# Two decoder layers on one core: the last Strassen product's weight forms emitted earlier, and half of a token tile scaled by ScalarE at the turn of the layers

## The chip, the cores and the metric

The kernel runs on one core of a Trainium2 chip. The metric is device time in microseconds (us) of one execution, given as the median of several runs. The names of the engines are those of the profile: PE is TensorE's matrix product, PEld its weight load, DVE is VectorE, ACT is ScalarE, POOL is GpSimd, SP issues most of the transfers.

## What is computed

Two layers (`DEPTH` = 2) of a decoder trunk on 512 tokens of width 1024, in float32. Cut to what matters here:

```
for l in range(DEPTH):
    a = hybrid_mixer(rms_norm(x, pre_mix_g[l]), ...)            # first product: h @ w_in[l]
    x = x + rms_norm(a, post_mix_g[l])
    c = memory_cross_attention(rms_norm(x, pre_xattn_g[l]), ...)
    x = x + rms_norm(c, post_xattn_g[l])
    hdn = jnp.square(jax.nn.relu(rms_norm(x, pre_mlp_g[l]) @ w_up[l]))   # width 4096
    x = x + rms_norm(hdn @ w_down[l], post_mlp_g[l])
```

`rms_norm(x, g)` is `x * rsqrt(mean(x*x) + 1e-6) * g`. The change lies in the last line, and in the step from there to the first line of the next layer ("the turn of the layers"): the residual x of the first layer is complete, is normalised and transposed, and feeds the second layer's product with `w_in`.

## The kernel before

The tokens are four tiles of 128 rows (t = 0 to 3), and each tile's 1024 columns are two halves of 512 (n = 0, 1). Every float32 operand of a product is kept as a rounded part and a rest (`whi` and `wlo` of a weight, `fh` and `fl` of an activation, `xth` and `xtl` of the transposed input), and one logical product is three matmuls into one PSUM bank (lines 239 to 241: hi x rest, rest x hi, hi x hi). The rounded part is made by ACT and the rest by DVE.

**The down product.** `hdn @ w_down` runs in four passes `qd_` over the inner dimension. In each, a 2 x 2 block product is done with seven products of combined operands. `plan` lists the seven as (number p, PSUM tiles, first, last, destinations). For product p, `right_form(p, B[g])` makes the weight's form for each half g of the pass's inner dimension: where needed DVE subtracts two raw weight blocks into one (line 1036 for p = 4), then `parts_w` (lines 161 to 166) makes `whi` on ACT (line 164) and `wlo` on DVE (line 165). `finish(j)` adds the finished PSUM tile of token tile d + j to the running sums `acc[t][n]` on DVE (line 1104). In the last pass (`end`) the order of `plan` is 1, 2, 5, 6, 3, 7, 4, and a completed half of `acc` goes through `done(t, n)`: sum of squares on ACT (`sumsq`, line 372, output `mss`), times the gain on DVE (line 1042). Once both halves of a token tile are there, `add_post_norm` follows: a small DVE operation (`pnm`, line 417), a power on POOL (`pnr`, line 139), and two DVE operations that make the new residual (`xs`, line 420). Product 4 is the last of the pass. It completes tiles 2 and 3, and its matmuls are the ones named `we` at the end of a layer, 24 of them, for j = 0 and 1 and g = 0 and 1.

**The turn.** In the first layer `done` then stores the tile and calls `norm_x(nxh, nxl, t, "n1")` (lines 393 to 407): two sums of squares of `xs` on ACT (line 372), `n1m` on DVE (line 376), the power `n1r` on POOL (line 139), and the two halves `xn` = `xs` times `n1r`, both on POOL (line 405). `put_off` delays the transposes in the emitted program: `transposed` turns each half with four PE transposes (`tp`, line 224), and ACT and DVE split it into `xth` (line 201) and `xtl` (line 203). The second layer's first product (PSUM tiles `ptm`, one for each token tile) needs `xth` and `xtl` of its token tile and the split of `w_in` (`whi` line 192, `wlo` line 197, one 128 x 512 operation per half of a weight tile).

**What sets the order.** The program is emitted in the order of the Python code. A list scheduler of the framework then orders each engine's instructions ahead of time, from its own costs, and each engine runs its list in that order, waiting on semaphores. So the same emitted code can stand in another order on an engine than in the source. Two tiles of PSUM serve the transposes (`tp`), four the tiles `we` and `ptm`.

Of the kernel before, what the change touches and what calls it, by code (L numbers as in the profile page):

```python
# [15 lines left out]
AF = mybir.ActivationFunctionType  # L16
OP = mybir.AluOpType
# [28 lines left out]
def block_kernel(ctx: ExitStack, tc, x, mem, positions, rel_bias, w_in, q_norm_g, w_uq, kv_norm_g,  # L46
# [3 lines left out]
    nc = tc.nc  # L50
# [13 lines left out]
    def unit(name, shape=(128, 512), dt=F32):  # L64
        return un.tile(list(shape), dt, tag="u", name=name)

    def small(name, w):
        return sm.tile([128, 4], F32, tag="sm", name=name)[:, :w]
# [8 lines left out]
    xs = [[None, None] for _ in range(NT)]  # L77
# [133 lines left out]
    def put_off(key, us, fn):  # L211
        late.append((clk[0] + us, key, fn))
# [153 lines left out]
    def feat_major(*a, **k):  # L366
        run(feat_major_steps(*a, **k))

    def sumsq(src, ss, scale=1.0):
        w = src.shape[-1]  # L370
        junk = unit("junk", (128, w))
        nc.scalar.activation(junk, src, AF.Square, scale=scale, accum_out=ss)

    def row_rstd(ms, tag):
        m = small(tag + "m", 1)
        nc.vector.scalar_tensor_tensor(m, ms[0], EPS, ms[1], op0=OP.add, op1=OP.add)
        return rpow(m, tag)

    def transposed(xn, n, dests, t):

        tp = t_ps("tp")
        for j in range(4):
            transpose(tp[:, j * 128:(j + 1) * 128], xn[:, j * 128:(j + 1) * 128], ident)
        tpv = tp.rearrange("p (j c) -> p j c", j=4)
        w = 8 // len(dests)
        for i in range(0, 4, w):
            h, lo = dests[(n * 4 + i) // w]
            k0 = (n * 4 + i) % w
            mw = min(w, 4)
            split_from(h[:, k0:k0 + mw, t * 128:(t + 1) * 128],  # L390
                       lo[:, k0:k0 + mw, t * 128:(t + 1) * 128] if SPLIT else None, tpv[:, i:i + mw, :])

    def norm_x(h, lo, t, tag, fast=()):

        hv = (h[:, 0:4, :], h[:, 4:8, :])
        lv = (lo[:, 0:4, :], lo[:, 4:8, :]) if SPLIT else (None, None)
        ms = small(tag + "ms", 2)
        for n in range(2):
            sumsq(xs[t][n], ms[:, n:n + 1], scale=1.0 / 32.0)
        r = row_rstd((ms[:, 0:1], ms[:, 1:2]), tag)  # L400
        xns = []
        for n in range(2):
            xn = unit("xn")
            eng = nc.vector if n in fast else nc.gpsimd
            eng.tensor_scalar(xn, xs[t][n], r[:, 0:1], 1.0, op0=OP.mult, op1=OP.mult)
            xns.append(xn)
        put_off(("xt", t), DELAY, lambda: [transposed(xns[n], n, list(zip(hv, lv)), t) for n in range(2)])

# [150 lines left out]
    for l in range(DEPTH):  # L559

        if l == 0:
            xth, xtl = new_xt()
            with tc.high_priority():
                norm_x(xth, xtl, 0, "n1", fast=(1,))
                ensure(("xt", 0))
            idle_products(10)

# [304 lines left out]
        xth, xtl = new_xt()  # L872
# [99 lines left out]
        xth, xtl = new_xt()  # L972
# [26 lines left out]
        nxh = nxl = None  # L999
# [25 lines left out]
        def right_form(p, b):  # L1025


            b11, b12, b21, b22 = b
            if p == 5:
                nc.vector.tensor_sub(b11, b12, b11)  # L1030
            elif p == 6:
                nc.vector.tensor_sub(b11, b22, b11)
            elif p == 7:
                nc.vector.tensor_sub(b12, b22, b12)
            elif p == 4:
                nc.vector.tensor_sub(b11, b21, b11)
            return parts_w({1: b11, 5: b11, 6: b11, 2: b21, 7: b12, 3: b22, 4: b11}[p])

        def done(t, n):

            sumsq(acc[t][n], ss[t][:, n:n + 1], scale=1.0 / 32.0)
            nc.vector.tensor_mul(acc[t][n], acc[t][n], gb[n])
            ready_halves[t] += 1
            if ready_halves[t] < 2:
                return
            add_post_norm(acc[t], ss[t], t, out[0] if l == DEPTH - 1 else None)
            if l < DEPTH - 1:
                store_x(t, xsave)
                norm_x(nxh, nxl, t, "n1")

        ready_halves = [0] * NT

        for qd_ in range(4):
            if qd_ == 3 and l < DEPTH - 1:
                nxh, nxl = new_xt()
            F = {p: [] for p in range(1, 8)}
            for g in range(2):
                ra = pp.tile([128, 1280], F32, tag="P", name="ra", bufs=2)[:, 0:1024]
                rb = pp.tile([128, 1280], F32, tag="PT", name="rb", bufs=2)[:, 0:1024]
                ra, rb = [r.rearrange("p (k c) -> p k c", k=2) for r in (ra, rb)]  # L1060

                def ev_up(m, ps, ra=ra, rb=rb):
                    r = (ra, rb)[m // 2][:, m % 2, :]
                    nc.scalar.activation(r, ps, AF.Relu)
                    nc.scalar.activation(r, r, AF.Square)

                feat_major(w_up[l], (qd_ * 2 + g) * 512, 4, NK, G_MLP + 8 * l, xh_f, xl_f, S, ev_up,
                           whole=2 if qd_ == 0 and g == 0 else 0)
                left_forms(F, ra, rb)
            B = [[raw_w(w_down[l], qd_ * 1024 + g * 512 + r * 256, 2, n * 512, 512)  # L1070
                  for r in range(2) for n in range(2)] for g in range(2)]
            A = [pss.tile([128, 512], F32, tag="s", name="wa") for _ in range(2)]
            C = [pst.tile([128, 512], F32, tag="t", name="wc") for _ in range(2)]
            E = [None] * 2
            end = qd_ == 3


            plan = ((1, A, True, False, ((0, 0),)), (5, C, True, False, ((2, 1),)),
                    (6, A, False, False, ((0, 1),)), (2, E, True, True, ((0, 0),)),
                    (7, A, False, False, ((2, 1),)), (3, C, False, True, ((0, 1),)),  # L1080
                    (4, A, False, True, ((2, 0),)))
            if end:
                plan = ((1, A, True, False, ((0, 0),)), (2, E, True, True, ((0, 0),)),
                        (5, C, True, False, ((2, 1),)), (6, A, False, False, ((0, 1),)),
                        (3, C, False, True, ((0, 1),)), (7, A, False, True, ((2, 1), (2, 0))),
                        (4, E, True, True, ((2, 0),)))
            for p, ps, first, last, dsts in plan:
                if ps is E:
                    E[:] = [mm_ps("we") for _ in range(2)]

                def product(g, i, j, w):
                    c = slice(j * 128, (j + 1) * 128)
                    fh, fl = F[p][g]
                    mm(ps[j], fh[:, i, c], fl[:, i, c], w[0][:, i, :], w[1][:, i, :],
                       first and g + i == 0, g + i == 2, not first)

                def finish(j):
                    for d, n in dsts:
                        t = d + j
                        if acc[t][n] is None:  # L1100
                            acc[t][n] = unit("acc")
                            nc.vector.tensor_copy(acc[t][n], ps[j])  # L1102
                        else:
                            nc.vector.tensor_add(acc[t][n], ps[j], acc[t][n])
                        if end and p in (2, 3, 4) or end and p == 7 and n == 1:
                            done(t, n)

                if end and p == 4:
                    w = [right_form(p, B[g]) for g in range(2)]
                    for j in range(2):  # L1110
                        for g in range(2):
                            for i in range(2):
                                product(g, i, j, w[g])
                        finish(j)
                        flush()
                    continue
                for g in range(2):
                    w = right_form(p, B[g])
                    for i in range(2):
                        for j in range(2):  # L1120
                            product(g, i, j, w)
                if end and p == 1:
                    gb = row_bcast(post_mlp_g, l)
                for j in range(2):
                    finish(j)
                if end and p in (2, 5):
                    for t in ((0, 1) if p == 2 else (2, 3)):
                        load_x(t, xmid)
                flush()
        xth, xtl = nxh, nxl  # L1130
# [36 lines left out]
```

## Time and profile before

| | |
|---|---|
| median of 3 runs | 1558.0 us (1557.4 to 1561.02) |
| the profiled execution, own time | 1556.26 us |
| its span in the trace | 1554.5 us |
| PE busy | 1510.6 us, 97% of the span |
| DVE busy | 997.8 us, 64% |
| ACT busy | 818.0 us, 53% |
| POOL busy | 245.1 us, 16% |

Times below are microseconds from the start of the profiled span. The span is 1.8 us shorter than the execution's own time, which is 1.7 us below the median of the runs. A busy share is an average over stages; matmuls overlap by their pipelining, so that consecutive ones start 0.23 us apart although one is listed with 0.39 us. [...]

### The profile page before, as it was taken

How to read it: one execution, taken by the hardware profiler on the slowest of the kernel's cores; microseconds unless marked ns; L12 is line 12 of the kernel's file. 1: busy time of each engine (PE TensorE's matmuls, PEld its weight loads, DVE VectorE, ACT ScalarE, POOL GpSimd, SP SyncE). 2: the span in 40 equal slices, each digit the busy share in tenths (PEclk: the TensorE clock that was granted, in tenths of full speed). 3: DMA queues.
4: the chain of work that ended last, by engine and by line, in shares of the span. 5: the costliest groups of instructions: out<-in, count | busy, mean ns of one | idle time of the engine just before them, and what ended most of it. 6: DMA issues, size and time to landing. Idle time of an engine off the chain costs nothing.

```text
span 1554.5 us, 21284 instructions
## 1 busy us (share of the span) xinstructions
PE 1510.6 (97%) x7861; PEld 1264.8 (81%) x7861; DVE 997.8 (64%) x1780; ACT 818.0 (53%) x1574; POOL 245.1 (16%) x433
## 2 busy tenths in 40 slices
PE   8999999999999999999989999999999999999996
PEld 6777788898898888888768877978988988888885
DVE  5555766456449677685974667654554695949577
ACT  5355766355356364645544566654554554645453
POOL 2133621021020000000121355201111100000000
PEclk9999999999999999999999999999999999999998
DMA  6432223513131506051631322243322324150512
GB/s 237 140 116 69 88 72 105 191 55 122 55 109 57 183 18 190 28 176 48 196 114 51 121 92 79 69 156 129 109 82 68 123 80 137 39 178 14 190 64 72
DMA packets 87404, 164.09 MB, mean 106 GB/s; under 512 B 6230, under 2 KB 12036, under 8 KB 87300
## 3 DMA queue, kind: packets, MB, share of 16 engines
q1 hardware_dynamic: 86724, 161.68, 31.9%
q8 instruction: 62, 1.02, 0.3%
q10 hardware_dynamic: 576, 1.05, 0.2%
q14 instruction: 42, 0.34, 0.1%
HBM read 154.29 MB, written 11.03 MB: 106 GB/s over the span
## 4 chain that ended last, share of the span: by engine, by line
PE 84%; DVE 7%; issue 3%; ACT 2%; DMA 2%; POOL 1%; SPq 0%; DVEq 0%; POOLq 0%; ACTq 0%
PE pfm L240 12%; PE pfm L239 12%; PE pfm L241 12%; PE ptm L239 6%; PE ptm L240 6%; PE ptm L241 6%; PE wa L239 3%; PE wa L240 3%; PE wa L241 3%; PE op L230 3%; PE sp L464 3%; DVE wlo L197 2%; PE ptp L224 2%; PE wc L240 2%; PE wc L241 2%
## 5 line engine op out<-in xcount | busy, mean ns | idle before, releaser
L240 PE MATMUL pfm<-xth,wlo 128*128 128x512 f32 (+1 forms) x896 | 322.4, 360 | 0.6
L239 PE MATMUL pfm<-xtl,whi 128*128 128x512 f32 (+1 forms) x896 | 322.2, 360 | 0.0
L241 PE MATMUL pfm<-xth,whi 128*128 128x512 f32 (+1 forms) x896 | 321.6, 359 | 0.0
L197 DVE SCALAR_TENSOR_TENSOR wlo<-raw,gT,whi 128x512 fp32r<-128x512 f32 (+3 forms) x332 | 229.9, 732 | 131.4 <-ACT whi L192 129.7
L192 ACT ACTIVATE whi<-raw,gT 128x512 fp32r<-128x512 f32 (+2 forms) x324 | 208.9, 697 | 179.8 <-PE pfm L241 87.3
L164 ACT ACTIVATE whi<-raw 128x1024 fp32r<-128x1024 f32 x112 | 118.1, 1060 | 143.0 <-PE pfm L241 52.8
L240 PEld LDWEIGHTS pfm<-xth,wlo 128*128 128x128 f32 x896 | 169.2, 189 | 27.0 <-DVE wlo L197 1.4
L241 PEld LDWEIGHTS pfm<-xth,whi 128*128 128x128 f32 x896 | 169.2, 189 | 25.5 <-issue 0.5
L239 PEld LDWEIGHTS pfm<-xtl,whi 128*128 128x128 f32 x896 | 169.2, 189 | 25.0
L165 DVE TENSOR_TENSOR wlo<-raw,whi 128x1024 fp32r<-128x1024 f32 x112 | 135.0, 1219 | 34.3 <-ACT whi L164 34.3
L139 POOL TENSOR_TENSOR pnr<-pnm,mhalf 128x1 f32<-128x1 f32 x24 | 17.2, 715 | 828.6 <-DVE pnm L417 828.6
L472 POOL TENSOR_SCALAR P<-P,rs 128x128 f32<-128x128 f32 (+3 forms) x128 | 71.4, 562 | 149.3 <-DVE rs L471 78.8
L239 PE MATMUL wa<-wlo,fh 128*128 128x512 f32 x240 | 93.6, 390 | 0.5 <-DVE acc L1102 0.5
L240 PE MATMUL wa<-whi,fl 128*128 128x512 f32 x240 | 93.4, 389 | 0.0
L241 PE MATMUL wa<-whi,fh 128*128 128x512 f32 x240 | 93.4, 389 | 0.0
L470 ACT ACTIVATE P<-P,nm 128x128 f32<-128x128 f32 (+3 forms) x128 | 71.1, 557 | 32.1 <-DVE nm L468 31.3
L185 DVE TENSOR_TENSOR wlo<-raw,whi 128x1024 fp32r<-128x1024 f32 x32 | 39.1, 1223 | 59.3 <-ACT whi L184 58.6
L239 PE MATMUL ptm<-wlo,xth 128*128 128x512 f32 (+2 forms) x192 | 68.3, 357 | 2.2 <-DVE wlo L197 1.8
L184 ACT ACTIVATE whi<-raw 128x1024 fp32r<-128x1024 f32 x32 | 33.9, 1061 | 67.2 <-PE ptm L241 64.5
L240 PE MATMUL ptm<-whi,xtl 128*128 128x512 f32 (+2 forms) x192 | 67.0, 349 | 0.2 <-DVE xtl L203 0.2
L241 PE MATMUL ptm<-whi,xth 128*128 128x512 f32 (+2 forms) x192 | 66.4, 346 | 0.0
L224 PE MATMUL ptp<-ident,P 128*128 128x128 f32 x320 | 50.4, 281 | 4.3 <-ACT PT L491 2.3
(248 smaller groups left out, 3286.9 us busy)
## 6 DMA issues: line engine op xcount, KB each, us to landing
raw<-in_w_up SPq DMA_DIRECT2D x64, 512.0 KB, 4.7
raw<-in_w_down SPq DMA_DIRECT2D x64, 512.0 KB, 4.1
raw<-in_w_in SPq DMA_DIRECT2D x24, 512.0 KB, 4.9
raw<-in_w_xk SPq DMA_DIRECT2D x16, 512.0 KB, 4.7
raw<-in_w_xv SPq DMA_DIRECT2D x16, 512.0 KB, 3.7
raw<-in_w_mix_out SPq DMA_DIRECT2D x16, 512.0 KB, 4.5
raw<-in_w_xq SPq DMA_DIRECT2D x16, 512.0 KB, 6.4
raw<-in_w_xo SPq DMA_DIRECT2D x16, 512.0 KB, 4.2
```

Source lines behind the costliest of these rows:

```text
L164: nc.scalar.activation(hi, raw, AF.Copy)
L165: nc.vector.tensor_sub(lo, raw, hi.bitcast(F32))
L192: weight_parts[:] = [nc.scalar.activation(cols(hi, k, False), cols(raw, k, True), AF.Copy, scale=g).ins]
L197: nc.vector.scalar_tensor_tensor(lv, rv, g, hv, op0=OP.mult, op1=OP.subtract)
L224: ins = nc.tensor.transpose(out_, in_, ident_)
L230: nc.tensor.matmul(ps, lhsT=lhsT, rhs=rhs, start=start, stop=stop)
L239: nc.tensor.matmul(ps, lhsT=lh, rhs=rl, start=first, stop=False, skip_group_check=more)
L240: nc.tensor.matmul(ps, lhsT=ll, rhs=rh, start=False, stop=False, skip_group_check=more)
L241: nc.tensor.matmul(ps, lhsT=lh, rhs=rh, start=False, stop=last, skip_group_check=more)
L464: nc.tensor.matmul(sp[:, :L], lhsT=q[:, i * 128:(i + 1) * 128], rhs=k[:, :L], start=n == 0, stop=n == len(parts) - 1)
L470: nc.scalar.activation(Pi, Pi, AF.Exp, bias=nm[:, i:i + 1], scale=-1.0, accum_out=rs[:, i:i + 1])
L472: nc.gpsimd.tensor_scalar(Pi, Pi, rs[:, i:i + 1], 1.0, op0=OP.mult, op1=OP.mult)
```

## The change

It does two things. In the last pass the two forms of product 4 are emitted behind the matmuls of product 7 and ahead of product 7's `finish`, instead of at the head of product 4. And `norm_x` takes an argument that says who scales the second half: at the turn of the layers that is ACT now (`nc.scalar.activation` with `scale=r`), POOL keeps the first half. At the start of the kernel DVE scales the second half as before; the other calls of `norm_x` keep POOL for both.

```diff
-    def norm_x(h, lo, t, tag, fast=()):
+    def norm_x(h, lo, t, tag, help=None):
...
             xn = unit("xn")
-            eng = nc.vector if n in fast else nc.gpsimd
-            eng.tensor_scalar(xn, xs[t][n], r[:, 0:1], 1.0, op0=OP.mult, op1=OP.mult)
+            if n == 1 and help is nc.scalar:
+                nc.scalar.activation(xn, xs[t][n], AF.Copy, scale=r[:, 0:1])
+            else:
+                eng = nc.gpsimd if n == 0 or help is None else help
+                eng.tensor_scalar(xn, xs[t][n], r[:, 0:1], 1.0, op0=OP.mult, op1=OP.mult)
             xns.append(xn)
...
-                norm_x(xth, xtl, 0, "n1", fast=(1,))
+                norm_x(xth, xtl, 0, "n1", help=nc.vector)
...
-                norm_x(nxh, nxl, t, "n1")
+                norm_x(nxh, nxl, t, "n1", help=nc.scalar)
...
                 if end and p == 4:
-                    w = [right_form(p, B[g]) for g in range(2)]
                     for j in range(2):
                         for g in range(2):
                             for i in range(2):
-                                product(g, i, j, w[g])
+                                product(g, i, j, last_w[g])
                         finish(j)
                         flush()
                     continue
...
                     for i in range(2):
                         for j in range(2):
                             product(g, i, j, w)
+                if end and p == 7:
+                    last_w = [right_form(4, B[g]) for g in range(2)]
```

On the engines' own lists, the change shows at three places. Lines of the changed kernel are 3 higher here (1104 is now 1107).

First place, the turn of the layers, PE. `we` are the two PSUM tiles of product 4 (we_7296 and we_7297 before, we_7306 and we_7307 now), `wlo_7300` and `wlo_7305` are the rests of its forms for g = 0 and g = 1 (wlo_7288 and wlo_7293 now), and `tp_7345`, `tp_7352` are the transposes of token tile 0. Before:

```order
L241 MATMUL we_7296<-whi_7299,fh_6802 128x512
L239 MATMUL we_7297<-wlo_7300,fh_6802 128x512
L240 MATMUL we_7297<-whi_7299,fl_6803 128x512
L224 MATMUL tp_7345<-ident_95,xn_7223 128x128 x4
L224 MATMUL tp_7352<-ident_95,xn_7225 128x128 x4
L241 MATMUL we_7297<-whi_7299,fh_6802 128x512
```

Now:

```order
L241 MATMUL we_7306<-whi_7287,fh_6802 128x512
L239 MATMUL we_7306<-wlo_7293,fh_6978 128x512
L240 MATMUL we_7306<-whi_7292,fl_6979 128x512
L241 MATMUL we_7306<-whi_7292,fh_6978 128x512
L239 MATMUL we_7306<-wlo_7293,fh_6978 128x512
L240 MATMUL we_7306<-whi_7292,fl_6979 128x512
L241 MATMUL we_7306<-whi_7292,fh_6978 128x512
L224 MATMUL tp_7345<-ident_95,xn_7223 128x128 x4
L224 MATMUL tp_7352<-ident_95,xn_7225 128x128 x4
L239 MATMUL we_7307<-wlo_7288,fh_6802 128x512
```

The transposes of tile 0 stood behind 8 of the 24 matmuls of product 4 and stand behind 12 now, and the 12 use the form of g = 1 for 6 of them. On DVE at the same place (`acc` are the additions of finished products, `xs_7082` and `xs_7084` the new residual of tile 0), before:

```order
L420 SCALAR_TENSOR_TENSOR xs_7084<-acc_5240,pnr_7208,xs_7084 128x512
L1104 TENSOR_TENSOR acc_5202<-wa_6998,acc_5202 128x512
L1104 TENSOR_TENSOR acc_5384<-wa_6998,acc_5384 128x512
L376 SCALAR_TENSOR_TENSOR n1m_7219<-n1ms_7214 128x1
L1104 TENSOR_TENSOR acc_5204<-wa_6999,acc_5204 128x512
L1104 TENSOR_TENSOR acc_5386<-wa_6999,acc_5386 128x512
L165 TENSOR_TENSOR wlo_7305<-raw_6990,whi_7304 128x1024
L1042 TENSOR_TENSOR acc_5242<-acc_5242,gb_7035 128x512
```

Now:

```order
L423 SCALAR_TENSOR_TENSOR xs_7084<-acc_5240,pnr_7208,xs_7084 128x512
L165 TENSOR_TENSOR wlo_7293<-raw_6990,whi_7292 128x1024
L376 SCALAR_TENSOR_TENSOR n1m_7219<-n1ms_7214 128x1
L1107 TENSOR_TENSOR acc_5202<-wa_6998,acc_5202 128x512
L1107 TENSOR_TENSOR acc_5384<-wa_6998,acc_5384 128x512
L1107 TENSOR_TENSOR acc_5204<-wa_6999,acc_5204 128x512
L1045 TENSOR_TENSOR acc_5242<-acc_5242,gb_7035 128x512
```

The rest of the form for g = 1 moved ahead of product 7's four additions, one of which now stands behind the next two rows. `n1m` of tile 0 has one long instruction ahead of it instead of two shorter ones.

Second place, DVE some ten instructions later: `wlo_7415` is the rest of the first tile of `w_in`, two operations for its two halves. Before:

```order
L1104 TENSOR_TENSOR acc_5386<-we_7297,acc_5386 128x512
L197 SCALAR_TENSOR_TENSOR wlo_7415<-raw_7412,gT_86,whi_7414 128x512 x2
L1042 TENSOR_TENSOR acc_5202<-acc_5202,gb_7035 128x512
L1042 TENSOR_TENSOR acc_5204<-acc_5204,gb_7035 128x512
L1042 TENSOR_TENSOR acc_5384<-acc_5384,gb_7034 128x512
```

Now:

```order
L1107 TENSOR_TENSOR acc_5386<-we_7307,acc_5386 128x512
L197 SCALAR_TENSOR_TENSOR wlo_7415<-raw_7412,gT_86,whi_7414 128x512
L1045 TENSOR_TENSOR acc_5202<-acc_5202,gb_7035 128x512
L1045 TENSOR_TENSOR acc_5204<-acc_5204,gb_7035 128x512
L1045 TENSOR_TENSOR acc_5384<-acc_5384,gb_7034 128x512
L420 SCALAR_TENSOR_TENSOR pnm_7324<-mss_4634 128x1
L203 TENSOR_TENSOR xtl_6629<-tp_7359,xth_6628 128x4x128
L423 SCALAR_TENSOR_TENSOR xs_7126<-acc_5384,pnr_7326,xs_7126 128x512
L423 SCALAR_TENSOR_TENSOR xs_7128<-acc_5202,pnr_7326,xs_7128 128x512
L203 TENSOR_TENSOR xtl_6629<-tp_7366,xth_6628 128x4x128
L197 SCALAR_TENSOR_TENSOR wlo_7415<-raw_7412,gT_86,whi_7414 128x512
```

The second half of the first weight tile's rest moved behind eight instructions: the three multiplications by the gain, `pnm`, tile 1's two `xtl` and tile 2's two `xs`. The second layer's first product needs it.

Third place, the end of the second layer, DVE. Before:

```order
L420 SCALAR_TENSOR_TENSOR xs_14157<-acc_12313,pnr_14289,xs_14157 128x512
L1104 TENSOR_TENSOR acc_12273<-wa_14067,acc_12273 128x512
L1104 TENSOR_TENSOR acc_12455<-wa_14067,acc_12455 128x512
L1104 TENSOR_TENSOR acc_12275<-wa_14068,acc_12275 128x512
L1042 TENSOR_TENSOR acc_12273<-acc_12273,gb_14104 128x512
L1104 TENSOR_TENSOR acc_12457<-wa_14068,acc_12457 128x512
L1042 TENSOR_TENSOR acc_12275<-acc_12275,gb_14104 128x512
L165 TENSOR_TENSOR wlo_14348<-raw_14059,whi_14347 128x1024
L1104 TENSOR_TENSOR acc_12455<-we_14339,acc_12455 128x512
```

Now:

```order
L423 SCALAR_TENSOR_TENSOR xs_14157<-acc_12313,pnr_14289,xs_14157 128x512
L165 TENSOR_TENSOR wlo_14336<-raw_14059,whi_14335 128x1024
L1107 TENSOR_TENSOR acc_12273<-wa_14067,acc_12273 128x512
L1107 TENSOR_TENSOR acc_12455<-wa_14067,acc_12455 128x512
L1107 TENSOR_TENSOR acc_12275<-wa_14068,acc_12275 128x512
L1045 TENSOR_TENSOR acc_12273<-acc_12273,gb_14104 128x512
L1107 TENSOR_TENSOR acc_12457<-wa_14068,acc_12457 128x512
L1045 TENSOR_TENSOR acc_12275<-acc_12275,gb_14104 128x512
L1107 TENSOR_TENSOR acc_12455<-we_14349,acc_12455 128x512
L1107 TENSOR_TENSOR acc_12457<-we_14350,acc_12457 128x512
```

The rest of the form for g = 1 moved ahead of six DVE instructions; PE's own list is unchanged there (12 matmuls with the form of g = 0, then 12 with that of g = 1). On ACT the four `xn` operations stand at the turn, each behind the `whi` half that follows the tile's sums of squares; on SP one weight load moved behind two stores of the residual.

## Rows read from the trace of the kernel before

**Rows 1.** The page's first line: the span.
```profile
span 1554.5 us, 21284 instructions
```

**Rows 2.** Busy time by stretch: length, engines PE to POOL, PEclk, DMA share, GB/s.
```profile
760.00:780.00 20.00, 16.71 (x70) 13.11 (x68) 16.69 (x26) 12.03 (x25) 5.97 (x7) 0.91 0.72 229
780.00:800.00 20.00, 16.06 (x71) 12.21 (x72) 18.18 (x29) 10.04 (x25) 10.32 (x10) 0.91 0.55 165
...
1520.00:1554.00 34.00, 20.93 (x84) 16.47 (x83) 25.30 (x37) 8.53 (x17) 3.49 (x4) 0.86 0.17 62
```

**Rows 3.** Waits, 760 to 812 us: total, times, longest.
```profile
PE tp L224 <- POOL xn L405: 6.9, 7, 2.0
```

**Rows 4.** Timeline of PE at the turn: start, us, instruction, count, [idle before].
```profile
768.23 0.39 PE L239 MATMUL we<-wlo,fh 128*128 128x512 f32 x1
...
771.22 0.66 PE L224 MATMUL tp<-ident,xn 128*128 128x128 f32 x4 [1.02 <-POOL xn L405]
773.37 1.11 PE L224 MATMUL tp<-ident,xn 128*128 128x128 f32 x4 [1.49 <-POOL xn L405]
...
775.14 0.63 PE L240 MATMUL we<-whi,fl 128*128 128x512 f32 x1
...
781.22 0.66 PE L224 MATMUL tp<-ident,xn 128*128 128x128 f32 x4 [2.00 <-POOL xn L405]
782.84 0.66 PE L224 MATMUL tp<-ident,xn 128*128 128x128 f32 x4 [0.96 <-POOL xn L405]
...
797.58 0.66 PE L224 MATMUL tp<-ident,xn 128*128 128x128 f32 x4 [0.44 <-POOL xn L405]
```

**Rows 5.** Timeline of DVE at the turn.
```profile
768.40 1.28 DVE L1104 TENSOR_TENSOR acc<-wa,acc 128x512 f32<-128x512 f32 x2
769.60 0.15 DVE L376 SCALAR_TENSOR_TENSOR n1m<-n1ms 128x1 f32<-128x1 f32 x1
...
770.86 1.38 DVE L165 TENSOR_TENSOR wlo<-raw,whi 128x1024 fp32r<-128x1024 f32 x1
...
773.99 1.42 DVE L420 SCALAR_TENSOR_TENSOR xs<-acc,pnr,xs 128x512 f32<-128x512 f32 x2
777.90 0.69 DVE L1104 TENSOR_TENSOR acc<-we,acc 128x512 f32<-128x512 f32 x1 [2.50 <-PE we L241]
...
779.11 0.15 DVE L376 SCALAR_TENSOR_TENSOR n1m<-n1ms 128x1 f32<-128x1 f32 x1
...
793.60 0.74 DVE L197 SCALAR_TENSOR_TENSOR wlo<-raw,gT,whi 128x512 fp32r<-128x512 f32 x1
```

**Rows 6.** Line 405 on POOL, 760 to 812 us: ns shortest/median/longest, first and last start.
```profile
L405 POOL TENSOR_SCALAR xn<-xs,n1r x8: 693/1217/2177, 770.5 to 796.4; 128x512 f32<-128x512 f32 x8
```

**Rows 7.** Timeline of ACT at the turn.
```profile
774.52 0.60 ACT L201 ACTIVATE xth<-tp 128x512 fp32r<-128x512 f32 x1 [2.01 <-PE tp L224]
775.02 2.55 ACT L192 ACTIVATE whi<-raw,gT 128x512 fp32r<-128x512 f32 x4
```

**Rows 8.** Waits of SP's queue, 820 to 900 us: total, times, longest.
```profile
SPq L157 <- DVE wlo L197: 55.2, 11, 17.2
```

**Rows 9.** Timeline of PE at the end of the kernel.
```profile
1540.99 0.57 PE L239 MATMUL we<-wlo,fh 128*128 128x512 f32 x1 [4.67 <-DVE wlo L165]
```

**Rows 10.** Timeline of DVE at the end.
```profile
1536.13 1.88 DVE L1104 TENSOR_TENSOR acc<-wa,acc 128x512 f32<-128x512 f32 x3
...
1539.73 1.21 DVE L165 TENSOR_TENSOR wlo<-raw,whi 128x1024 fp32r<-128x1024 f32 x1
1543.73 0.69 DVE L1104 TENSOR_TENSOR acc<-we,acc 128x512 f32<-128x512 f32 x1 [2.79 <-PE we L241]
...
1549.38 1.42 DVE L420 SCALAR_TENSOR_TENSOR xs<-acc,pnr,xs 128x512 f32<-128x512 f32 x2 [0.66 <-POOL pnr L139]
```

**Rows 11.** Timeline of POOL at the end.
```profile
1530.78 0.92 POOL L139 TENSOR_TENSOR pnr<-pnm,mhalf 128x1 f32<-128x1 f32 x1 [313.19 <-DVE pnm L417]
...
1548.80 0.55 POOL L139 TENSOR_TENSOR pnr<-pnm,mhalf 128x1 f32<-128x1 f32 x1 [2.20 <-DVE pnm L417]
```

## The prediction

> **What bounds the kernel now.** I read the page, then busy time by stretch, then the waits and timelines of the two stretches where PE is not full. The page gives a span of 1554.5 [rows 1], and PE is busy 97% of it, so only the places where PE waits, or runs at the lower clock, can give time. Two lie where the diff is. At the turn of the layers (760 to 800) PE is busy 16.71 + 16.06 of 40 us, 7.2 idle, and the granted clock is 0.91 [rows 2]. [...] In the last 34 us PE is busy 20.93 [rows 2]; the rest is a wait and the tail behind the last matmul.
>
> Who is waited for: at the turn PE's transposes wait 6.9 us in seven waits for `xn`, which POOL scales [rows 3]. The timeline shows the form of it. Each tile costs two waits, one for each half: 1.02 and 1.49 for tile 0, 2.00 and 0.96 for tile 1 [rows 4]. Between the first half and the second lies POOL's second operation, which takes between 0.69 and 2.18 us [rows 6]. At the end PE waits once, 4.67 us, for `wlo` [rows 9]: the form for g = 1, which DVE begins at 1539.73 behind six other operations [rows 10].
>
> **The change at the end of the kernel.** Nothing is added here; one DVE operation moves. Before, four additions and two multiplications run from 1536.13 to 1539.73, 3.6 us, and then the form, 1.2 us, and PE starts at 1540.99 [rows 9, 10]. Now the form runs first: 1536.13 + 1.2 = 1537.3, and PE starts at about 1537.4. It had been idle since 1540.99 - 4.67 = 1536.3, so its wait is 1.1. Its 12 matmuls take 12 x 0.23 = 2.7 at the full clock and end at 1540.1. The six operations follow the form on DVE and end at 1537.3 + 3.6 = 1540.9, later than PE. So the stall goes from PE to DVE, and DVE is late next: the first addition of product 4 starts at 1540.9 and not at 1543.73 [rows 10], 2.8 earlier.
>
> The tail from that addition to the last pair of `xs` (1549.38) was 5.65 [rows 10]. It keeps its instructions, but the second tile's addition and multiplication now stand ahead of the first tile's pair. In the old list the last pair waited for that multiplication behind the first pair, so the tail loses one operation of 0.6. Gain: 2.8 + 0.6 = 3.4. Against it, POOL's power `pnr` now runs beside a DVE multiplication. Alone it took 0.55; 1530.78 has one of 0.92 [rows 11]. That costs 0.4 if it happens. I take 3.3, between 2.5 and 3.6.
>
> [...]
>
> **The change at the turn, first step.** The form for g = 1 follows tile 0's `xs`, where two additions started at 768.40 [rows 5]. So it ends at 768.4 + 1.2 = 769.6. PE starts product 4 at 768.23 [rows 4]; six matmuls, 0.23 apart, are through at 769.6, and the seventh needs the form. It arrives just in time (0.1 lost), and the 12 end at 771.05. `n1m` of tile 0 was at 769.60 [rows 5] and stays there, since one operation of 1.2 replaces two of 0.6. So the first half of `xn` is ready when it was: its transposes start at 771.2, with a wait of 0.2 instead of 1.02. The second half runs on ACT beside it: a scaled copy of that shape takes 2.55 / 4 = 0.64 there [rows 7], so it is ready first, and the wait of 1.49 is gone. Eight transposes take 0.8, the other 12 matmuls 2.7: product 4 ends at 774.8. Before, PE was through with it at 781.22 - 2.00 = 779.2 [rows 4]. Gain so far: 4.4. Part of it is clock: before, the matmuls behind the two waits started 0.43 apart (one at 775.14, listed 0.63 long [rows 4]), the low level.
>
> **Second step, tile 1.** Its `n1m` was at 779.11 [rows 5], because its sums of squares on ACT stood behind four roundings of `w_in`, started at 775.02, and these behind an `xth` that waited 2.01 for PE [rows 7]. Now one rounding stands ahead of the sums and that wait is gone. Following the lists: three additions to 771.4, ACT's sum to 771.7, multiplication, `pnm`, power to 773.2, `xs` to 774.5 (before: from 773.99 to 775.4 [rows 5]), sums on ACT to 775.9, `n1m` at 776.0, 3.1 earlier. From `n1m` to the transpose it was 1.6 for tile 0 (769.60 to 771.22) and 2.1 for tile 1 (779.11 to 781.22) [rows 4, 5]. So tile 1's transposes start at 777.6 to 778.1. PE idles some 3 us, as much as before in its two waits of 2.00 and 0.96; the wait is not removed here, it comes 3 to 4 us earlier. The clock falls behind it as it did: I charge eight transposes and five matmuls at half speed, 1.5 to 2.
>
> **Third step, a new wait.** The second half of `wlo_7415` stands behind eight more DVE instructions now. Counting the list from `n1m` at 776.0: `xtl` and an addition to 777.2, the first half 0.67, three multiplications to about 779.8 (each waits for a sum on ACT), `pnm` and `xtl` to 780.5, `xs` after its power to 782.0, `xtl`, the half: 783.4 to 784. PE reaches the matmul that needs it at 781.3 to 782, so it waits about 2 us, where it had no wait. From here DVE paces PE. The last half of `wlo` of these four weight tiles began at 793.60 [rows 5]; by the list it begins between 789.0 and 790.0, 3.6 to 4.6 earlier, and the last tile's transposes follow (before: 797.58 [rows 4]), their `xn` half on ACT saving the last wait of 0.44. Two more matmuls stand behind them than before, 0.45. So when the turn is over, what is left is 3.6 to 5.3. I take 4.4. ACT's four added operations, 4 x 0.64 = 2.6, I cost at nothing beyond these steps: ACT is busy 22 of the 40 us [rows 2], and the idle 18 hide them. Where they are exposed instead is the fourth rival.
>
> What follows does not give it back: the next weight loads wait 55.2 us in all for DVE to free buffers [rows 8], so they come earlier along with DVE, and the load that moved behind two stores belongs to a later product.
>
> **Sum.** 4.4 + 3.3 = 7.7. The profiled execution took 1556.3 (span 1554.5 and 1.8 around it), so it would take 1548.6. It lies 1.7 below the median of the runs, 1558.0; the median becomes 1550.3.
>
> **Rivals.** First: the turn gives nothing, because DVE sets its length whoever else is faster. For it speaks that DVE is busy 34.9 of 40 us there [rows 2] and that a new wait for `wlo` appears; if DVE idled as before, only 0.4 to 1 would come from less contention. Against it, 2.50 of DVE's idle time there is one wait for product 4 [rows 5], which the first step removes, and 1 more lies in waits on POOL. Then the end alone counts: 1558.0 - 3.3 = 1554.7.
>
> Second: less low clock than I charge. If PE's wait for tile 1 stays short enough that neither the transposes nor the matmuls slow down, another 2 come: 1548.
>
> Third: the end gives nothing. If DVE's six operations and the power take as long as PE did, only the turn counts: 1553.6. The row against it is the wait of 2.79 of DVE for PE [rows 10], which is free time now.
>
> Fourth, slower: ACT in its new place. It runs its list in order: the roundings at 775.02 had their data long before and stood behind a waiting `xth` [rows 7]. Each `xn` on ACT waits for DVE's `n1m` and POOL's power, and behind it stand sums of squares that DVE waits for. Price: 0.9 to 1.9 for the wait (power of 0.55 to 0.92 [rows 11] and what lies around it) and 0.64 for the operation, 1.5 to 2.5 for each of four tiles, 6 to 10 in all if nothing hides it; with 3 more for PE at the low clock through the stretch, 1550.3 + 13 = 1563. It decides from 7.7 on, that is, if nearly all of it is exposed. Against it: while ACT waits for the power, DVE has additions that need nothing from ACT. [...]
>
> **Chances.** My sum 0.62, first rival 0.16, second 0.12, third 0.07, fourth 0.03. A measurement of this kernel can tell about 0.3%, 4.7 us, from no change: faster means below 1553.3. The sum's own range is 1548 to 1553, all of it faster but 0.02; with the second rival and a small part of the third, faster is 0.75; the first rival and most of the third make no change, 0.22; the fourth, 0.03. The range for 8 in 10 reaches from the second rival to the first: 1546.5 to 1555.2.
>
> **What the profile would show.** Right: no wait between the two halves' transposes of a tile at the turn; the `we` matmuls done 4 us earlier; a PE wait near 1.1 at the end, and the first `we` addition bound by DVE. Wrong: the form for g = 1 arriving after PE's sixth matmul by more than 1 us, a wait for `wlo` of more than 4 at the turn, or ACT idle in front of `xn` with sums behind it that DVE waits for.

## The result and the profile after

The changed kernel takes 1550.4 us (median of 4 runs, 1546.4 to 1551.81) against 1558.56 for the kernel before on the same chip, where a fourth run has joined the three that gave 1558.0. The ratio, taken over all runs, is 0.9941, 95% interval 0.9919 to 0.9964; the two medians alone give 0.9948. The forecast was 1550.3. The profiled execution is the slowest of the four (1551.81, mean granted clock 0.989; the fastest, 1546.4, had 0.995). Lines of the changed kernel stand three higher: the addition is L1107, the gain L1045, `pnm` L420, `xs` L423; `xn` is L408 on POOL and L405 on ACT.

Span of the profiled execution, the page's first line [rows 1]:

```profile
span 1550.0 us, 21290 instructions
```

One span can't be compared with another to 1 us here: where no edit lies, executions differ too. I therefore cut each trace at three starts of PE. The **lead** ends at the first `we` matmul of the first layer, the **turn** at the first `pfm` matmul of the second layer, the **middle** at the first `we` of the second layer, and the **end** is what remains.

| kernel | lead | turn | middle | end | span |
|---|---|---|---|---|---|
| before | 768.23 | 43.03 | 722.18 | 21.06 | 1554.5 |
| after | 769.97 | 39.07 | 723.17 | 17.79 | 1550.0 |

Turn and end give 3.96 + 3.27 = 7.23; lead and middle, which in the profiles of this study lie between 766.6 and 771.4 and between 721.3 and 724.1 with the same work in them, took 2.73 back in this one execution. The medians lie 8.2 apart.

Busy time by stretch of the changed kernel, columns as in [rows 2], where PEclk is the granted clock of TensorE as a share of full speed:

```profile
760.00:780.00 20.00, 17.63 (x86) 14.13 (x84) 18.87 (x29) 12.40 (x26) 4.50 (x6) 1.00 0.78 258
780.00:800.00 20.00, 17.09 (x75) 13.17 (x74) 16.49 (x29) 11.58 (x27) 5.07 (x6) 0.91 0.57 173
```

PE is busy 34.7 of the 40 us instead of 32.8, and the first 20 us run at a granted clock of 1.00 (0.91 before [rows 2]). The waits of PE from 760 to 812 us (total, times, longest) answer to [rows 3]:

```profile
PE tp L224 <- POOL xn L408: 2.4, 1, 2.4
PE ptm L239 <- DVE wlo L197: 2.0, 1, 2.0
PE ptm L239 <- ACT xth L201: 0.5, 1, 0.5
PE ptm L240 <- DVE xtl L203: 0.4, 1, 0.4
```

Seven waits of 6.9 for POOL's `xn` became one of 2.4, and a wait of 2.0 for `wlo`, that was not there, stands behind it. PE's timeline at the turn, which answers to [rows 4], shows where:

```profile
769.97 0.39 PE L239 MATMUL we<-wlo,fh 128*128 128x512 f32 x1
...
771.41 0.50 PE L239 MATMUL we<-wlo,fh 128*128 128x512 f32 x1
...
772.91 1.09 PE L224 MATMUL tp<-ident,xn 128*128 128x128 f32 x8
...
776.36 0.39 PE L241 MATMUL we<-whi,fh 128*128 128x512 f32 x1
779.12 1.09 PE L224 MATMUL tp<-ident,xn 128*128 128x128 f32 x8 [2.37 <-POOL xn L408]
779.97 0.48 PE L239 MATMUL ptm<-wlo,xth 128*128 128x512 f32 x1
...
785.07 0.50 PE L239 MATMUL ptm<-wlo,xth 128*128 128x512 f32 x1 [2.01 <-DVE wlo L197]
...
787.50 0.63 PE L241 MATMUL ptm<-whi,xth 128*128 128x512 f32 x1
```

The eight transposes of tile 0 and of tile 1 now go in one piece each (x8), tile 0's without a wait. PE is through with the `we` matmuls where its wait for tile 1 begins, at 779.12 - 2.37 = 776.75, which is 6.78 after the first; before, it was 779.22 - 768.23 = 10.99 [rows 4]. Matmuls of 0.63, which start 0.43 apart, stand only between 785.4 and 788.8, behind the new wait; the granted clock of that stretch is 0.50 (the low level below), and 1.00 (the full level) from 769.97 to 776.70, where they start 0.23 apart.

At the end, PE's one wait, which answers to [rows 9], is 1.09:

```profile
1536.18 0.50 PE L239 MATMUL we<-wlo,fh 128*128 128x512 f32 x1 [1.09 <-DVE wlo L165]
...
1538.81 0.39 PE L241 MATMUL we<-whi,fh 128*128 128x512 f32 x1
```

DVE's timeline there, against [rows 10]:

```profile
1534.91 1.22 DVE L165 TENSOR_TENSOR wlo<-raw,whi 128x1024 fp32r<-128x1024 f32 x1
1536.05 1.88 DVE L1107 TENSOR_TENSOR acc<-wa,acc 128x512 f32<-128x512 f32 x3
...
1539.64 1.28 DVE L1107 TENSOR_TENSOR acc<-we,acc 128x512 f32<-128x512 f32 x2
...
1541.79 0.68 DVE L1045 TENSOR_TENSOR acc<-acc,gb 128x512 f32<-128x512 f32 x1
1542.91 1.41 DVE L423 SCALAR_TENSOR_TENSOR xs<-acc,pnr,xs 128x512 f32<-128x512 f32 x2 [0.44 <-POOL pnr L139]
```

The form goes first; the additions of product 4 follow the six operations without a wait (before, 2.79 of waiting for PE), and PE's last matmul has ended 0.4 before they start. POOL's power, against [rows 11]:

```profile
1541.95 0.93 POOL L139 TENSOR_TENSOR pnr<-pnm,mhalf 128x1 f32<-128x1 f32 x1 [8.41 <-DVE pnm L420]
1544.48 0.55 POOL L139 TENSOR_TENSOR pnr<-pnm,mhalf 128x1 f32<-128x1 f32 x1 [1.59 <-DVE pnm L420]
```

The first of the two started while DVE multiplied (at 1541.79), and took 0.93; the second had no DVE operation beside it, and took 0.55.

### The profile page after: what moved, and what is told of

It is laid out like the page before. It is cut to its first block, busy times and chain, and to the rows that moved or that the text cites. A ratio compares the mean times of both kernels' runs of the same rounds, so it can differ in the third digit from the quotient of the medians.

```text
span 1550.0 us, 21290 instructions
## 1 busy us (share of the span) xinstructions
PE 1509.1 (97%) x7861; PEld 1265.6 (82%) x7861; DVE 995.9 (64%) x1780; ACT 820.0 (53%) x1578; POOL 239.0 (15%) x429
## 4 chain that ended last, share of the span: by engine, by line
PE 84%; DVE 7%; issue 3%; ACT 2%; DMA 2%; POOL 1%; SPq 0%; DVEq 0%; POOLq 0%; ACTq 0%
PE pfm L240 12%; PE pfm L239 12%; PE pfm L241 12%; PE ptm L239 6%; PE ptm L240 6%; PE ptm L241 6%; PE wa L239 3%; PE wa L240 3%; PE wa L241 3%; PE sp L467 3%; PE op L230 3%; DVE wlo L197 2%; PE ptp L224 2%; PE wc L240 2%; PE wc L239 2%
```

## The experiments

All are edits of the changed kernel. Ratios are to the kernel before, on the same chip and taken along with it. Turn and end are cut as above, each from one execution. Of two executions with the same lists one turn was 0.85 longer than the other, and in another pair 0.74 (both below), so smaller differences of the turn show nothing by themselves. The end varies by 0.14 among the five kernels that have the same list there.

| kernel | turn | end | span | median | ratio, 95% interval |
|---|---|---|---|---|---|
| after | 39.07 | 17.79 | 1550.0 | 1550.4 | 0.9941, 0.9919 to 0.9964 |
| forms alone | 39.13 | 17.77 | 1550.0 | 1549.99 | 0.9953, 0.9937 to 0.9968 |
| ACT alone | 39.59 | 21.37 | 1553.3 | 1554.69 | 0.9978, 0.9967 to 0.9988 |
| second half on DVE | 39.99 | 17.91 | 1550.8 | 1552.32 | 0.9965, 0.9952 to 0.9977 |
| both halves on ACT | 36.59 | 17.89 | 1545.2 | 1547.48 | 0.9933, 0.9915 to 0.995 |
| forms ahead of product 7 | - | - | 1555.0 | 1555.58 | 0.9981, 0.9968 to 0.9995 |
| gain on POOL | 38.63 | 17.01 | 1549.5 | 1548.21 | 0.9942, 0.9919 to 0.9965 |
| gain left out | 36.55 | 17.01 | 1541.4 | 1547.18 | 0.9934, 0.9915 to 0.9954 |
| both on ACT, gain on POOL | 37.21 | 16.85 | 1548.0 | 1545.33 | 0.9936, 0.991 to 0.9961 |
| halves swapped | 39.92 | 17.82 | 1548.0 | 1549.82 | 0.9939, 0.9926 to 0.9953 |
| both on ACT, gain on POOL at the end | 37.33 | 16.99 | 1549.8 | 1547.6 | 0.9935, 0.9922 to 0.9947 |

**Forms alone.** The scaling stays on POOL, both halves.

```diff
-                norm_x(nxh, nxl, t, "n1", help=nc.scalar)
+                norm_x(nxh, nxl, t, "n1")
```

> Only the forms of product 4 are emitted ahead; POOL scales both halves of the tile as before. DVE's and PE's lists are those of the changed kernel. Two stretches are read from the trace: the turn, from the first matmul of product 4 in the first layer to the first matmul of the second layer's q product (43.0 us before, 39.1 with the change), and the end, from the first matmul of product 4 in the second layer to the end of the span (21.1 and 17.8). If each edit has a share of the turn (the prediction's first step: the second half on ACT takes a wait of 1 to 1.5 us away): end 17.8, turn 40.5 to 42, time about 1553. If DVE alone sets the turn's length (first rival, turned round): end 17.8, turn 39.1, time as with the whole change, 1550.

The turn took 39.13, the end 17.77: all of the change's gain that one execution can show, 3.90 and 3.29, without ACT. PE's timeline:

```profile
772.85 1.31 PE L224 MATMUL tp<-ident,xn 128*128 128x128 f32 x8
778.89 0.66 PE L224 MATMUL tp<-ident,xn 128*128 128x128 f32 x4 [1.97 <-POOL xn L408]
780.50 0.66 PE L224 MATMUL tp<-ident,xn 128*128 128x128 f32 x4 [0.96 <-POOL xn L408]
...
785.05 0.50 PE L239 MATMUL ptm<-wlo,xth 128*128 128x512 f32 x1 [2.00 <-DVE wlo L197]
```

Tile 0 has no wait here either. Its second half is still on POOL, but the two halves take 1.36 together, where in the kernel before the second half alone took 2.18. POOL before, beside DVE's form of 770.86 [rows 5]:

```profile
771.14 2.18 POOL L405 TENSOR_SCALAR xn<-xs,n1r 128x512 f32<-128x512 f32 x1
```

POOL and DVE with the forms alone:

```profile
772.10 1.36 POOL L408 TENSOR_SCALAR xn<-xs,n1r 128x512 f32<-128x512 f32 x2
```

```profile
771.29 1.88 DVE L1107 TENSOR_TENSOR acc<-wa,acc 128x512 f32<-128x512 f32 x3
```

DVE beside them now adds product 7 out of PSUM. Tile 1 does wait twice, 2.93 in all instead of 2.37, and that costs nothing: PE reaches the new wait for `wlo` sooner or later, and leaves it at 785.05 as in the changed kernel (785.07, with leads of 769.92 and 769.97).

**ACT alone.** The last forms are made where they were, behind product 7.

```diff
                 if end and p == 4:
+                    last_w = [right_form(p, B[g]) for g in range(2)]
...
-                if end and p == 7:
-                    last_w = [right_form(4, B[g]) for g in range(2)]
```

> Only the second half on ACT at the turn; the forms of product 4 stay at the head of product 4, so PE's and DVE's lists are those of the kernel before. If each edit has a share: end 21.1 as before, turn 40 to 42, since the four waits for the second half (1.49, 0.96, 0.56, 0.44) go, time about 1556. If the order of DVE does it alone: turn 43, time 1558. If ACT's queue in its new place costs what the fourth rival says: turn above 43, time above 1558.

The end stays at 21.37 (before 21.06), so it belongs to the forms alone. But the turn took 39.59, 3.44 less than before and below the 40 to 42 expected. Each edit by itself gives nearly the whole gain of the turn, and both together 3.96, not 7.3. Here DVE's list is that of the kernel before, with `wlo_7415` in one piece, and PE's waits for `wlo` are 0.15 and 0.64; its waits for `xn` are 1.01, 3.33 and 0.42. PE's timeline:

```profile
771.45 1.09 PE L224 MATMUL tp<-ident,xn 128*128 128x128 f32 x8 [1.01 <-POOL xn L408]
...
779.54 1.95 PE L224 MATMUL tp<-ident,xn 128*128 128x128 f32 x8 [3.33 <-POOL xn L408]
```

What the two edits share is the front of the turn. Each one puts tile 0's transposes in one piece, which takes away the wait of 1.49 and the low clock behind it (0.52 from 774.2 to 776.8 before; `we` matmuls 0.43 apart there, 0.23 apart behind tile 0's transposes in both kernels here): PE is through with product 4 7.75 after its first matmul (779.54 - 3.33 - 768.46) with ACT alone and 7.00 (778.89 - 1.97 - 769.92) with the forms alone, against 10.99 before and 6.78 with both. What limits behind it differs: with the forms it is the wait of 2.00 for `wlo`, with ACT alone tile 1's `xn`, 3.33, whose half on POOL took 1.67 beside DVE's two `wlo`.

**Second half on DVE.** `help=nc.vector` instead of `nc.scalar`.

> The whole change, but DVE scales the second half instead of ACT. If DVE paces the turn, as the third step of the prediction says, four more operations of 0.3 to 0.7 us on DVE lengthen it by 0.5 to 2.5: turn 39.6 to 41.6, end 17.8, time 1551 to 1553. If ACT's wait for POOL's power with DVE's sums behind it is what limits the turn now, it becomes shorter: turn 37 to 39, time 1548 to 1550.

The turn took 39.99, 0.9 more than with ACT, within the expected range; the end is 17.91. Four operations of 0.49 on the engine that paces are 1.9 of work; 0.9 came out on PE, which is no more than the turn varies between executions.

**Gain on POOL; gain left out.** Both take two multiplications by the gain off DVE, in either layer. The second one doesn't do them at all, so its result lacks that gain for the second half of tiles 2 and 3.

```diff
-            nc.vector.tensor_mul(acc[t][n], acc[t][n], gb[n])
+            (nc.gpsimd if t >= 2 and n == 1 else nc.vector).tensor_tensor(acc[t][n], acc[t][n], gb[n], op=OP.mult)
```

```diff
-            nc.vector.tensor_mul(acc[t][n], acc[t][n], gb[n])
+            if not (t >= 2 and n == 1):
+                nc.vector.tensor_mul(acc[t][n], acc[t][n], gb[n])
```

> The whole change, and the multiplication by the gain of the second halves of tiles 2 and 3 (two in each layer) is done by POOL instead of DVE. DVE has two operations of 0.6 us less at the turn and at the end, and the scheduler puts both halves of the first weight tile's rest together again. If DVE paces both stretches: end 17.8 less up to 1.2 (16.6 to 17.2), turn 39.1 less 1 to 3 (36 to 38), time 1546 to 1548. If POOL's longer operation and its clash with DVE's operations on the same tiles cost as much: turn 39 to 40, end 17.8 to 18.5, time 1550 to 1551.

> The whole change; the multiplication by the gain of the second halves of tiles 2 and 3 is left out in both layers (the computation is changed by that), so DVE has the two operations of 0.6 less and POOL is not loaded in their place. e8 with POOL gave a turn of 38.6 and an end of 17.0. If DVE paces both stretches and POOL's clash took e8's gain back: turn 36.5 to 38, end 16.5 to 16.8. If DVE's load is not what sets the turn (the waits for POOL's power and the transposes do): turn 38.5 to 39.1, end 17.

Left out, 1.2 of DVE's work takes 2.5 off the turn (36.55), and PE no longer waits for `wlo` at all: in this stretch it waits twice for POOL's `xn`, 2.37 and 1.04. So DVE did pace the turn. But 2.5 is more than the work left out, and the list moved with it: three halves of `wlo` go ahead of the one gain that is left, where the changed kernel has one half ahead of three gains. On POOL the same removal gives 0.4, between the two ranges expected and less than a turn can tell. DVE's timeline of the kernel with the gain on POOL shows why:

```profile
779.70 3.21 DVE L197 SCALAR_TENSOR_TENSOR wlo<-raw,gT,whi 128x512 fp32r<-128x512 f32 x3
782.83 1.78 DVE L1045 TENSOR_TENSOR acc<-acc,gb 128x512 f32<-128x512 f32 x1
```

And POOL's:

```profile
780.66 3.39 POOL L1045 TENSOR_TENSOR acc<-acc,gb 128x512 f32<-128x512 f32 x2 [0.66 <-ACT junk L372]
```

While POOL multiplies, three operations that take 2.07 in the changed kernel take 3.21, and a multiplication of 0.69 takes 1.78: DVE lost 2.2 to save 1.2. At the end both give 17.01 (16.5 to 16.8 was expected of leaving it out): there POOL's time is hidden, and 0.8 is gained either way.

**Both halves on ACT.**

```diff
-            if n == 1 and help is nc.scalar:
+            if help is nc.scalar:
```

> The whole change, but ACT scales both halves at the turn, POOL keeps the powers alone. Four more operations of 0.6 to 0.7 us on ACT, and no long POOL operation beside DVE's at the turn. If DVE paces the turn: 38 to 39.1, end 17.8, time 1549 to 1551. If ACT in its new place begins to limit (fourth rival), each tile's transposes come 0.6 later: turn 40 to 41.5, time 1551 to 1553.

The turn took 36.59, below both ranges expected and 2.5 less than in the changed kernel, and the stretch from 768.5 to 798.5 runs at clock 1.00 (0.94 there in the changed kernel). Tile 1's transposes do come 0.57 later (9.72 after the first `we`, 9.15 in the changed kernel), as was expected if ACT's queue limits, but the turn is not longer for it. PE's timeline:

```profile
778.03 0.66 PE L224 MATMUL tp<-ident,xn 128*128 128x128 f32 x4 [2.81 <-ACT xn L405]
...
784.62 0.50 PE L239 MATMUL ptm<-wlo,xth 128*128 128x512 f32 x1 [0.62 <-DVE wlo L197]
```

and DVE's:

```profile
777.11 2.07 DVE L197 SCALAR_TENSOR_TENSOR wlo<-raw,gT,whi 128x512 fp32r<-128x512 f32 x3
779.24 1.92 DVE L1045 TENSOR_TENSOR acc<-acc,gb 128x512 f32<-128x512 f32 x3
```

Besides the clock, two things differ from the changed kernel: POOL has no scaling left, and the lists came out otherwise. Three halves of `wlo` now go ahead of the three gains, where the changed kernel has one. PE does 18 `ptm` matmuls before it stops for `wlo`, against 6.

**Halves swapped.** This tries one of the two, and only in part: the first half goes to ACT, the second to POOL, so POOL still has one operation for each tile. The lists of all engines are those of the changed kernel, row for row.

```diff
-            if n == 1 and help is nc.scalar:
+            if n == 0 and help is nc.scalar:
...
-                eng = nc.gpsimd if n == 0 or help is None else help
+                eng = nc.gpsimd if n == 0 or help in (None, nc.scalar) else help
```

> The first half on the scalar engine and the second on the vector pool's neighbour, GpSimd: the lists of all engines stay those of the changed kernel, row for row, only the two halves of each tile change places. Theory 'the order of the lists': with both halves on the scalar engine the turn took 36.6 because the vector engine's list has both halves of the last split weights together ahead of the gains; with the changed kernel's list the turn stays at 39 (38.6 to 39.6), with a wait of about 2 for the last split weights. Rival 'GpSimd late on the first half': the turn falls by at least 1.2 to 37.8 or less and that wait shrinks below 1, since the first half no longer waits for GpSimd. Span and median of the changed kernel within 0.3% for the first theory, 1.2 to 2.5 us faster for the second.

The turn took 39.92. The rival's 37.8 is out; the list's 39 (38.6 to 39.6) is missed by 0.3, on the high side. PE's timeline:

```profile
775.73 1.09 PE L224 MATMUL tp<-ident,xn 128*128 128x128 f32 x8 [2.37 <-ACT xn L405]
...
777.35 0.63 PE L241 MATMUL ptm<-whi,xth 128*128 128x512 f32 x1
...
781.70 0.79 PE L239 MATMUL ptm<-wlo,xth 128*128 128x512 f32 x1 [1.52 <-DVE wlo L197]
...
786.56 0.63 PE L240 MATMUL ptm<-whi,xtl 128*128 128x512 f32 x1
```

The wait of 2.37 is the same to the hundredth. But here the matmuls behind it run at the low level, 0.43 apart in place of 0.23, from 776.6 to 787, and the clock of 768.5 to 798.5 is 0.83. PE takes longer over the six matmuls, so its wait for `wlo` is 1.52 instead of 2.01. DVE begins its three gains 9.70 after the first `we`, as in the changed kernel (9.71): the pace of DVE is that of its list. So which half is on POOL is not what holds the changed kernel back. At tile 1 it could hardly be: in the changed kernel POOL's half ends at 779.07 and ACT's at 779.03.

**Forms ahead of product 7.** `p == 3` instead of `p == 7` in the condition that makes the last forms.

> The whole change, but the forms of product 4 are emitted behind product 3, ahead of product 7's own forms. DVE's list then has the two subtractions and two rests of product 4 ahead of the rests of product 7, and the additions of product 3 and tile 0's residual between. If DVE paces, PE now waits 5 to 7 us for product 7 and has no wait at product 4 in either layer: time 1553 to 1560. If earlier is simply better, the wait of 1.1 at the end goes and the time is 1548 to 1550.

It gave back most of the gain, 0.9981, with the time in the expected range but not by the expected wait: at the end PE waits 0.34 for product 7's form, not 5 to 7. PE's list turned round: product 4 stands ahead of product 7, so the cuts above don't apply. The last matmul is now one of product 7 (`wa`, started at 1541.18), and behind it stand the additions of both products:

```profile
1540.93 1.89 DVE L1107 TENSOR_TENSOR acc<-wa,acc 128x512 f32<-128x512 f32 x3 [2.43 <-PE wa L241]
...
1544.53 1.29 DVE L1107 TENSOR_TENSOR acc<-we,acc 128x512 f32<-128x512 f32 x2
```

From the last matmul's start to the end of the span it is 13.8, against 1550.0 - 1538.81 = 11.2 in the changed kernel.

**Two combinations.** Both halves on ACT with the gain on POOL in either layer, and with the gain on POOL in the last layer alone (`t >= 2 and n == 1 and l == DEPTH - 1`).

> Both halves scaled by ACT, and POOL does the gain of the second halves of tiles 2 and 3: a try at a version that beats both kernels. If DVE paces: turn 37.5 to 38.6, end 17.0, time 1547 to 1549. If POOL's operation holds up its powers or DVE: turn 39 to 40.5, end 17.0, time 1550.

> The two parts that were best in their own segment, put together: both halves on the scalar engine at the turn (turn 36.6 there), and the gain of the last two tiles' second half on GpSimd in the last layer alone (end 17.0 there). If the segments are independent: turn 36.6, end 17.0, about 3.3 below the changed kernel in the sum of the segments, median about 1547, ratio 0.991 to 0.994 to the kernel before. Rival: they are not, since the list of the last layer ahead of the end moves too; then one of the segments shows it by more than 0.5.

Turn and end add up to 54.06 and 54.32, against 56.86 in the changed kernel and 54.48 with both halves on ACT alone. The parts are independent as far as the end goes (16.85, 16.99). The turn of the second is 37.33 where the same lists gave 36.59: here PE ran at the low level (matmuls 0.43 apart) from 781.1 to 786.7, while DVE began its three gains 10.93 after the first `we` in both. So one execution's turn is known to about 0.7. These two and both halves on ACT alone were not measured along with the changed kernel, so their medians don't compare with its own; by ratio the three are 0.9933 to 0.9936 against 0.9941, about 1 us, and the intervals overlap. That they are better, by 2.4 to 2.8, is shown by the segments of one execution each, and not by the whole time.

## Why the prediction was right, point by point

**The end: right in mechanism and size.** Predicted 3.3, between 2.5 and 3.6; measured 3.27, and 3.29 with the forms alone. The wait of 1.1 is 1.09, and DVE is late next, as said. The term for POOL's power (0.4 if it happens) is what was seen: 0.93 against 0.55. The sum can be followed part by part: the first addition of product 4 came 2.86 earlier after the first `we` (7.43 instead of 10.29; 2.8 worked out), and from there to the last `xs` it took 5.42 instead of 5.65, so the tail lost 0.23, about the 0.6 less the 0.38 of the power. The longer power, at 1541.95, stood beside the multiplication of 1541.79; why it takes longer there no run shows. With that term the end was to give 3.0, without it 3.4; the two parts give 3.09. The rest of the 3.27, about 0.2, came behind the last `xs`, where the sum had no term. The third rival is out.

**The turn, first step: right in size, wrong in its cause.** The form arrives 0.1 late, product 4 is through 6.78 after its start (6.6 worked out), and 4.2 of the 4.4 is there. But the step gave the wait of 1.49 to ACT's help. The forms alone remove it as well, because POOL's second half is short there. What stands beside it differs: DVE's list behind `n1m` had two additions, then the form and a multiplication, and POOL took 2.18 for the half; it has three additions now, and POOL took 1.36 for both halves. I had both rows (0.69 and 2.18) and did not ask which of them the moved list would give.

**Second step: right, with the low clock in another place.** `n1m` of tile 1 came 7.52 after the first `we` (7.77 worked out, 10.88 before), and PE idled 2.37 (3). The low level was charged to the work right behind that wait, 1.5 to 2, at half speed; the trace has 0.43 in place of 0.23 between matmuls where the granted clock is 0.50. It came only behind the `wlo` wait, on some eight matmuls, 1.6. So the amount was met by chance, at another wait. With halves swapped the low level came where I had put it.

**Third step: right.** The second half of `wlo_7415` was done 15.04 after the first `we`, which is 783.3 on the time axis of before (783.4 to 784 worked out). The wait is 2.01 (2). The last half of `wlo` of the four tiles began on DVE at 791.4, which is 789.7 on that axis (789.0 to 790.0 worked out). DVE paces from there: in the changed kernel its row lists no wait between 774 and 787, and leaving out 1.2 of its work, with the list that this gave, shortened the turn by 2.5. What the step did not see is that this wait is where ACT's help goes. On top of the forms the help shows 0.06, which is nothing that a turn can tell, and the two edits are not additive: alone they give 3.90 and 3.44, together 3.96. Tile 3's wait of 0.44 is gone with the forms alone, too.

**Sum and rivals.** 7.7 predicted, 7.23 in the segments, 8.2 in the medians. That the median was met to 0.1 is luck: the four executions lie 5.4 apart. The turn's 3.96 lies in its range of 3.6 to 5.3, below the 4.4 taken. The first rival (the turn gives nothing) is out, although its mechanism, DVE setting the length, is real: it takes effect behind product 4, not before it. Its 0.4 to 1 for contention was an estimate; in the kernel before DVE's form took 1.38 beside POOL's scaling and three multiplications, partly beside it, 2.30; in the changed one, with POOL idle, they took 1.22 and 1.92. The second (less low clock) did not occur in the changed kernel's profiled execution; both halves on ACT show a turn with no low stretch, at 36.59, and gain on POOL another, at 38.63. The fourth, slower: ACT waited for POOL's power 1.8 in four waits, none over 0.7, and with twice the work on ACT the turn was the shortest of those that do the whole computation. With both halves on ACT tile 1 came 0.57 later, and the turn was not longer for it. The 3 charged for the low clock through the stretch was an estimate that no run shows; with halves swapped PE ran at the low level for 10 us, and the turn was 0.85 longer.

**What stays open.** Both halves on ACT changes the lists and takes POOL's remaining scaling away at once. Halves swapped shows that the place of the first half alone gives nothing; how much of the 1.7 to 2.5 is the list, how much is POOL's remaining operation gone and how much is the clock was not separated. For the list speaks that the kernel without the gain has three halves of `wlo` ahead as well, keeps the first half on POOL, and has the same turn (36.55); but it also has 1.2 less of DVE's work. Nor is it known what decides whether the low level follows a given wait.

## What to carry to other kernels

When two edits both remove the same wait, run each alone: here each alone gave most of the turn's gain, and ACT's help on top of the forms added nothing that could be measured, because the wait that it removes was gone already and the next one is for DVE. Before an operation is moved to another engine, read which instructions will stand beside it: POOL's second `xn` of tile 0 took 2.18 beside DVE's form, and with the form moved both halves took 1.36, without a new engine. Where an order is made by a planner, compare the lists of each version: the best turns came with lists that have three halves of `wlo` ahead of the gains, which no line of the edits mentions, and one emission placed too early turned PE's products round.

## What was unexpected in the hardware

Two multiplications of 128x512 on POOL took 1.7 each and cost DVE, beside them, nearly twice what it saved (2.2 against 1.2); at the end of the kernel (1520 to 1550) POOL was busy 6.50 in six operations, where the changed kernel has 3.87 in four, so 2.63 for two more, and the same move gained 0.8. The granted clock is not settled by the program alone: executions of the changed kernel had means of 0.989 to 0.995. And behind the same wait of 2.37 at the same place, the changed kernel and gain on POOL ran on at the full level (matmuls 0.23 apart), halves swapped and gain left out at the low one (0.43 apart), with halves swapped for 10 us. Its turn was only 0.85 longer; its one wait for DVE at the turn was 1.52, where the changed kernel has 2.01 and 0.41.
